# A two-layer hybrid encoder in fp32r: latent projections first and freed from the norm of x, first squares summed by TensorE, a searched order of instructions

## The chip, the cores and the metric

One core of one Trainium2 chip runs the whole program. The metric is the device time of one execution in microseconds (us). The kernel before was timed three times; its median is 1267.3 us. One execution was also profiled, and all rows below come from that one.

## The reference

Sequence 512, width 1024, two layers, all in float32. Each layer does, on x (512 x 1024):

```python
proj = rms_norm(x, attn_norm[l]) @ w_in[l]
h_mla, h_diff, h_ch = jnp.split(proj, [IN_MLA, IN_MLA + IN_DIFF], axis=-1)
o_mla = rms_norm(mla_attention(h_mla, ...), mla_out_norm[l])    # 6 heads, latents of 256 (q) and 128 (k, v)
o_diff = diff_attention(h_diff, ...)                            # 6 heads, two softmaxes each
o_ch = rms_norm(chunk_attention(h_ch, ...), chunk_out_norm[l])  # 4 heads
x = x + jnp.concatenate([o_mla, o_diff, o_ch], axis=-1) @ w_out[l]
x = x + conv_ffn(rms_norm(x, ffn_norm[l]), ...)                 # 2 x 2816 wide, causal conv of 3, silu gate
```

and a last `rms_norm`. In `mla_attention` the latents `c_q` and `c_kv` are normed a second time, `rms_norm(c_q, q_norm) @ w_uq`. That second norm takes the first one out again: with r the row factor of the first norm and a the raw product, `rms_norm(r a)` is `a / sqrt(mean(a²) + eps / r²)`, and `eps / r²` is `eps (mean(x²) + eps)`.

## The kernel before

x lies transposed: eight tiles `xs[k]` of 128 channels x 512 positions. Every float32 factor is split in two fp32r halves (high, and the rest), and every product is three fp32r matmuls: high x high, high x low, low x high. A weight unit of 128 output channels therefore takes 24 matmuls of 512 columns (`proj`, L748), which add into one of three PSUM banks named psproj.

The norm factor r of x is not in the operands. `Gain.split` (L712) makes the halves of gain times x, the matmuls run on them, and `unit` (L868) multiplies the finished bank by r when it empties it; until r is there the bank stays taken (`Gain.finish`, L732). r itself comes from `Gain.square` (L720): ScalarE (ACT) squares a tile, VectorE (DVE) adds it to a sum, and `rstd` (L671) splits the sum (`split_sums`), sums it over the partitions with two matmuls against ones into a bank named pspt, and `rsqrt` (L691) makes r from it: Ln, Exp and Square on ACT, two instructions on DVE.

Weights come as jobs in a fixed order (`ORDER`, L81): q0 and q1 are the query latents, kv the key/value latent, kr the rotary key; e, v, u, d, c, g are the other projections; a and b the two parts of the output projection. `weights` (L536) loads a raw tile over the sync queue (SP), ACT casts the high half, and the low half is made either by DVE (a subtraction) or by ACT and an adding DMA of GpSimd (POOL), `pool.dma_start(..., accum_op=ALU.add)`. Job v (unit "uv") and the jobs u need the normed latents; the first 384-wide matmuls of the program are those of uv, in `latent_values` (L988). `latent` (L967) empties a latent's bank with r and norms it again.

The order of the instructions is planned in the kernel itself. Every instruction is first recorded (`Engine.__getattr__`, L361, so nearly all rows carry L361 as their line), with a cost and with lags between engines (`Clock.issue`, `lag`). `Clock.emit` (L332) then schedules the record backwards and forwards four times and keeps the order whose last instruction starts earliest. Each engine executes its own queue in that order.

Of the kernel before, what the change touches and what calls it, by code (L numbers as in the profile page):

```python
# [40 lines left out]
for t, n in (("wh", 2), ("wl", 3), ("xg", 8), ("lat", 3), ("kmla", 4), ("x", 6), ("v", 5), ("pt", 2), ("nhl", 1)):  # L41
    RINGS_R[t] = list(range(NR, NR + n))
    NR += n
# [16 lines left out]
for t, w, n in (("wraw", 1024, 2), ("P", GCOLS, 2), ("P1", GCOLS, 1), ("ev", S, 2), ("rb", S, 1), ("acc", S, 1),  # L60
# [10 lines left out]
RINGS_F["set"] = (S, [ol0[0], o0[4], o0[5]])  # L71
# [4 lines left out]
ROUNDS = 4  # L76
# [4 lines left out]
ORDER = "q0 kv kr q1 e0 v e1 u0 u1 u2 d0 d1 d2 e2 c0 c1 g0 g1 a0 a1 a2 a3 a4 a5 a6 a7 b0 b1"  # L81
# [39 lines left out]
class Clock:  # L121
# [6 lines left out]
    TO_PE = dict(act=0.265, dve=0.252, pool=0.203, pe=0.0)  # L128

# [70 lines left out]
    def settle(self):  # L200
# [15 lines left out]
        while ready:  # L216
# [13 lines left out]
    def issue(self, eng, op, outs, ins, func, emit):  # L230
# [62 lines left out]
    def lag(self, a, eng):  # L293

        return 0.0 if a.eng == eng else self.TO_PE[a.eng] if eng == "pe" else 0.197 if a.eng == "pe" else 0.157 if eng == "pool" else 0.13

    def list_schedule(self, rank, needs, users, forth):
# [8 lines left out]
        for _ in self.ops:  # L306
# [11 lines left out]
            if o.size and forth:  # L318
                line = max(line, end + 0.65) + o.size / 360e3
            for d in users(o):  # L320
                a, b = (o, d) if forth else (d, o)
                if a.size:
                    r = line + 0.9 + o.late if forth else end + 1.55 + a.late + a.size / 360e3
# [8 lines left out]
    def emit(self):  # L332


        start = self.list_schedule(list(range(len(self.ops))), lambda o: o.needs, lambda o: o.users, True)
        best = start
        for _ in range(ROUNDS):
            back = self.list_schedule([-(start[o.n] + o.cost) for o in self.ops], lambda o: o.users, lambda o: o.needs, False)
            start = self.list_schedule([-(back[o.n] + o.cost) for o in self.ops], lambda o: o.needs, lambda o: o.users, True)
            best = min(best, start, key=max)  # L340
# [136 lines left out]
def encoder(ctx, tc, xT, pos_row, pos_col, wflat, small, lam, relx, cst, out):  # L477
# [58 lines left out]
    def weights(l, name, run, finish, gate=lambda: True):  # L536
        o, c = offs[l, name]
        runs = [(0, c // 2), (c // 2, c)] if l == 0 and not work.jobs else [(0, c)]
# [4 lines left out]
        def fetch():  # L543
            raw = T("wraw")
            part(raw, *runs[0])
            if len(runs) > 1:
                rest_of_first.append(lambda: part(raw, *runs[1]))
            return raw

        def halves(raw):  # L550
# [8 lines left out]
            for a, b in runs:  # L559
                act.copy(wh[:, a:b], raw[:, a:b])  # L560
# [941 lines left out]
```

## Time and profile before

| | |
|---|---|
| runs | 1266.69, 1267.3, 1270.7 us; median 1267.3 |
| the profiled execution | 1264.97 us, span of its instructions 1263.2 us |
| busy share of the span | PE 97%, weight loads 78%, DVE 70%, ACT 56%, POOL 10% |
| granted TensorE clock, mean | 0.99 of 2.4 GHz |
| the two attention parts | about 0 to 285 us and 625 to 901 us |
| the two gated MLPs | about 285 to 625 us and 901 to 1250 us |

The profiled execution is 2.3 us below the median. PE's busy share counts a matmul from its start to its modelled end, so matmuls overlap in it, and a stretch at 100% need not be at TensorE's peak; the number of matmuls in a stretch tells more.

### The profile page before, as it was taken

How to read it: one execution, taken by the hardware profiler on the slowest of the kernel's cores; microseconds unless marked ns; L12 is line 12 of the kernel's file. 1: busy time of each engine (PE TensorE's matmuls, PEld its weight loads, DVE VectorE, ACT ScalarE, POOL GpSimd, SP SyncE). 2: the span in 40 equal slices, each digit the busy share in tenths (PEclk: the TensorE clock that was granted, in tenths of full speed). 3: DMA queues.
4: the chain of work that ended last, by engine and by line, in shares of the span. 5: the costliest groups of instructions: out<-in, count | busy, mean ns of one | idle time of the engine just before them, and what ended most of it. 6: DMA issues, size and time to landing. Idle time of an engine off the chain costs nothing.

```text
span 1263.2 us, 15644 instructions
## 1 busy us (share of the span) xinstructions
PE 1219.3 (97%) x5591; PEld 990.1 (78%) x5591; DVE 882.3 (70%) x1608; ACT 710.9 (56%) x1224; POOL 127.7 (10%) x186
## 2 busy tenths in 40 slices
PE   6899999989999999999999999999999999999996
PEld 4788776768888888888877878777788888888885
DVE  7798899668776347775457979975877643677644
ACT  6798887755443134444367878976644422444443
POOL 1113320140000000000011143101300000000001
PEclk9899999999999999999999999999999999999998
DMA  6657961543232332323366597526232233323232
GB/s 183 145 143 150 232 139 42 130 117 102 98 101 81 99 107 96 101 90 92 103 144 140 134 219 172 123 68 162 89 101 94 86 95 118 95 92 100 78 100 90
DMA packets 51470, 146.86 MB, mean 116 GB/s; under 512 B 6464, under 2 KB 9536, under 8 KB 51392
## 3 DMA queue, kind: packets, MB, share of 16 engines
q1 hardware_dynamic: 36992, 106.27, 26.4%
q0 software_dynamic: 14400, 39.59, 16.9%
q8 instruction: 44, 0.72, 0.2%
q14 instruction: 34, 0.28, 0.1%
HBM read 104.16 MB, written 2.10 MB: 84 GB/s over the span
## 4 chain that ended last, share of the span: by engine, by line
PE 80%; DVE 9%; ACT 5%; DMA 3%; issue 1%; SPq 0%; DVEq 0%; ACTq 0%
PE psproj L361 70%; DVE af L361 5%; PE pss L361 4%; PE pspt L361 3%; DVE ar L361 3%; PE psav L361 3%; ACT ar L361 3%; ACT af L361 3%; DMA af<-in_wflat 2%; DVE xa L361 1%; DMA xa<-in_xT 0%; DMA ar<-af 0%; DVE rl L361 0%; SPq L361 0%; ACT L860 0%
## 5 line engine op out<-in xcount | busy, mean ns | idle before, releaser
L361 PE MATMUL psproj<-ar 128*128 128x512 f32 (+1 forms) x4595 | 1107.9, 393 | 25.4 <-ACT ar L361 9.0
L361 PEld LDWEIGHTS psproj<-ar 128*128 128x128 f32 x4595 | 852.6, 189 | 204.8 <-ACT ar L361 22.3
L361 ACT CAST ar<-af 128x1024 fp32r<-128x1024 f32 (+3 forms) x338 | 272.9, 822 | 222.6 <-PE psproj L361 194.7
L361 DVE TENSOR_TENSOR ar<-af,ar 128x512 fp32r<-128x512 f32 (+3 forms) x257 | 240.7, 939 | 174.1 <-ACT ar L361 173.4
L361 DVE SCALAR_TENSOR_TENSOR af<-af,sma 128x511 f32<-128x511 f32 (+1 forms) x192 | 143.0, 750 | 47.6 <-ACT af L361 44.3
L361 ACT ACTIVATE af<-af,sma 128x512 f32<-128x512 f32 x88 | 71.9, 818 | 141.5 <-DVE af L361 141.5
L361 POOL DMA_DIRECT2D ar<-af x62 | 54.7, 883 | 664.1 <-ACT ar L361 586.2
L361 ACT ACTIVATE af<-af,mn 128x128 f32<-128x128 f32 (+3 forms) x176 | 98.3, 559 | 16.8 <-DVE mn L361 16.1
L361 ACT ACTIVATE af<-af 128x512 f32<-128x512 f32 (+1 forms) x106 | 66.1, 624 | 66.5 <-DVE af L361 65.4
L361 PE MATMUL pss<-ar 128*128 128x128 f32 (+9 forms) x336 | 88.5, 338 | 2.2 <-DVE mn L361 2.1
L361 DVE TENSOR_TENSOR af<-psproj,af 128x512 f32<-128x512 f32 x114 | 77.9, 685 | 14.7 <-PE psproj L361 14.1
L361 DVE TENSOR_TENSOR af<-af 128x512 f32<-128x512 f32 (+1 forms) x78 | 52.9, 678 | 36.4 <-ACT af L361 35.6
L361 PEld LDWEIGHTS pss<-ar 128*128 128x128 f32 (+2 forms) x336 | 55.9, 188 | 22.0 <-DVE mn L361 7.7
L361 ACT ACTIVATE ar<-af 128x1024 fp32r<-128x1024 f32 (+3 forms) x62 | 59.1, 953 | 20.9 <-DMA af<-in_wflat 15.6
L361 PE MATMUL psav<-ar 128*128 128x512 f32 (+3 forms) x256 | 66.7, 334 | 2.7 <-DVE ar L361 1.9
L361 DVE TENSOR_TENSOR ar<-pspt,ar 128x512 fp32r<-128x512 f32 (+1 forms) x106 | 63.0, 606 | 4.3 <-ACT ar L361 2.7
L361 PE MATMUL pspt<-ident,af 128*128 128x128 f32 x360 | 63.6, 278 | 1.4 <-DVE af L361 1.1
L361 PEld LDWEIGHTS pspt<-ident,af 128*128 128x128 f32 x360 | 45.6, 141 | 18.3 <-DVE af L361 5.1
L361 DVE TENSOR_TENSOR xa<-xa,psproj 128x512 f32<-128x512 f32 (+1 forms) x65 | 43.1, 672 | 19.7 <-PE psproj L361 19.6
L361 PEld LDWEIGHTS psav<-ar 128*128 128x128 f32 x256 | 45.0, 189 | 12.0 <-DVE ar L361 4.3
L361 DVE CUSTOM_DVE_ANT_0 af<-pss,dist 128x384 f32<-128x384 f32 (+2 forms) x96 | 45.5, 484 | 5.1 <-PE pss L361 4.9
L361 POOL DMA_DIRECT2D ar<-ar x78 | 43.0, 588 | 35.3 <-PE pss L361 26.0
(65 smaller groups left out, 537.2 us busy)
## 6 DMA issues: line engine op xcount, KB each, us to landing
af<-in_wflat SPq DMA_DIRECT2D x127, 512.0 KB, 3.4
ar<-af POOLq DMA_DIRECT2D x38, 512.0 KB, 5.1
af<-in_wflat SPq DMA_DIRECT2D x48, 384.0 KB, 3.0
af<-in_wflat SPq DMA_DIRECT2D x38, 320.0 KB, 2.9
ar<-ar POOLq DMA_DIRECT2D x72, 128.0 KB, 4.8
ar<-af POOLq DMA_DIRECT2D x16, 384.0 KB, 4.2
xa<-in_xT SPq DMA_DIRECT2D x8, 256.0 KB, 5.7
af<-in_relx SPq DMA_DIRECT2D x8, 256.0 KB, 2.8
```

The lines of the kernel that those rows point to most:

```text
L361: self.clock.issue(self.name, op, outs, ins + aps, func, lambda: fn(*args, **kw))
```

## The change

- The latents go first: kv, q0, q1, then kr. Their banks are emptied by a plain ACT copy as soon as the matmuls are done, without r. In place of r, the second norm gets `eps / r²`: `rstd` and the new `squares` keep `me = EPS / d * sum(x²)` (an ACT copy of the PSUM sum), and DVE adds `d / P * me` to the sum of the latent's squares.
- In layer 0, DVE no longer adds the squares of x: each squared tile goes as a float32 matmul against ones into one PSUM bank, with one more for eps.
- The first three jobs of the program are loaded and split in halves, their high halves cast by DVE and their low halves subtracted by DVE; the first x tile is loaded ahead of the first weights. The ring of high halves grows from two tiles to three. The descriptor scratch of POOL's DMAs is halved.
- The last scaling of x is three DVE instructions for each half, in place of eight on DVE and POOL.
- The planner gets a lag between instructions of one engine (`SELF`), other prices for DMAs, and sixty rounds disturbed by random numbers in place of four; it keeps the order whose last instruction ends earliest.

```diff
-for t, n in (("wh", 2), ("wl", 3), ("xg", 8), ...
+for t, n in (("wh", 3), ("wl", 3), ("xg", 8), ...
...
-ROUNDS = 4
+ROUNDS = 60
...
-ORDER = "q0 kv kr q1 e0 v e1 u0 u1 u2 d0 d1 d2 e2 c0 c1 g0 g1 a0 a1 a2 a3 a4 a5 a6 a7 b0 b1"
+ORDER = "kv q0 q1 kr e0 v e1 u0 u1 u2 d0 d1 d2 e2 c0 c1 g0 g1 a0 a1 a2 a3 a4 a5 a6 a7 b0 b1"
...
+    SELF = dict(pe=0.0, act=0.14, dve=0.125, pool=0.3, sp=0.0)
...
-                o.line = free["line"] = max(free["line"], o.end + 0.65) + o.size / 360e3
-                o.end = o.line + 0.9 + o.late
+                o.line = free["line"] = max(free["line"], o.end + 0.65) + o.size / 300e3
+                o.end = o.line + 0.6 + o.late
...
-            late = (2.3 if size < 1 << 18 else 4.5) * (eng == "pool")
+            late = (2.6 if size < 1 << 18 else 1.8) * (eng == "pool")
...
+        rnd = random.Random(0)
+        best = start = forth([o.n for o in self.ops])
         for _ in range(ROUNDS):
...
+            late = back([rnd.gauss(0, 0.5) - start[o.n] - o.cost for o in self.ops])
+            start = forth([-(late[o.n] + o.cost) for o in self.ops])
+            best = min(best, start, key=span)
+            if span(start) > span(best) + 0.3:
+                start = best
...
-        runs = [(0, c // 2), (c // 2, c)] if l == 0 and not work.jobs else [(0, c)]
+        runs = [(0, c // 2), (c // 2, c)] if l == 0 and len(work.jobs) < 3 else [(0, c)]
...
-                act.copy(wh[:, a:b], raw[:, a:b])
-            if name[0] == "f" or clock.now() == 0:
+                (act.copy if len(runs) == 1 else dve.tensor_copy)(wh[:, a:b], raw[:, a:b])
+            if name[0] == "f" or len(runs) > 1:
...
+            if keep is not None:
+                act.activation(keep, pb, AF.Copy, scale=EPS / d)
...
+        def squares(self):
+
+            pb = PT("pt")
+            pe.matmul(pb, lhsT=ones.bitcast(F32), rhs=eps_t.to_broadcast([P, S]), start=True, stop=False)
+            for k in range(KD):
+                q = tmp("sq")
+                act.activation(q, self.xs[k], AF.Square)
+                pe.matmul(pb, lhsT=ones.bitcast(F32), rhs=q, start=False, stop=k == KD - 1)
+            self.me = tmp("me")
+            act.activation(self.me, pb, AF.Copy, scale=EPS / self.d)
+            self.then(rsqrt(pb, self.d, tmp("y"), tmp("s"), lambda: tmp("rb")))
...
-                rstd(self.acc, self.d, P, ones, self.then, "rb")
+                self.me = tmp("me")
+                rstd(self.acc, self.d, P, ones, self.then, "rb", keep=self.me)
...
-            def finish(job, acc, rb):
+            def finish(job, acc):
                 f = tmp("ol")
-                dve.tensor_tensor(f, acc, rb, op=ALU.mult)
+                act.copy(f, acc)
+                close_bank()
...
-                rstd(sumsq(fs), d, P, ones, then)
-            return unit(name, gain_a, finish)
+                acc = sumsq(fs)
+                dve.scalar_tensor_tensor(acc, gain_a.me, d / P, acc, op0=ALU.mult, op1=ALU.add)
+                rstd(acc, d, P, ones, then, eps=0.0)
+            return weights(l, name, lambda w: proj(gain_a.tiles, w, []), finish)
...
-        for k, eng in enumerate((dve, dve, pool, dve, dve, dve, pool, dve)):
-            x = xs[k][:, hs]
-            eng.tensor_tensor(x, x, r, op=ALU.mult)
-            if k in OUT:
-                x = xa.rearrange("p (k s) -> p k s", k=KD)[:, done : k + 1, hs]
-                sp.dma_start(out[:, done : k + 1, hs], x)
-                done = k + 1
+        for k in OUT:
+            x = tiles[:, done : k + 1, hs]
+            dve.tensor_tensor(x, x, r[:, None, :].to_broadcast([P, k + 1 - done, HALF]), op=ALU.mult)
+            sp.dma_start(out[:, done : k + 1, hs], x)
+            done = k + 1
...
-    nc = _bacc.Bacc("TRN2", target_bir_lowering=False, num_devices=1, dynamic_dma_scratch_size=8192)
+    nc = _bacc.Bacc("TRN2", target_bir_lowering=False, num_devices=1, dynamic_dma_scratch_size=4096)
```

What this does to the queues is shown at three places. In each row stand the instruction, what it writes and reads, and the shape it writes (`x12` is twelve of them in a row); ar are the fp32r tiles, af the float32 ones, xa is x, psproj, pspt and pss are PSUM banks.

PE at the start of layer 0, before: from the end of the second unit to the first 384-wide matmuls, which are uv's. Of the units, the three psproj banks hold q0, kv and kr first, then q1 (the first psproj_63 rows here) and e0 (psproj_64, 24).

```order
L361 MATMUL psproj_64<-ar 128x512 x13
L361 MATMUL pspt_68<-ar,ones 128x512
L361 MATMUL psproj_65<-ar 128x512 x12
L361 MATMUL pspt_68<-ar,ones 128x512
L361 MATMUL psproj_65<-ar 128x512 x4
L361 MATMUL psproj_63<-ar 128x512 x12
L361 MATMUL pspt_69<-ar,ones 128x512 x2
L361 MATMUL psproj_63<-ar 128x512 x12
L361 MATMUL psproj_64<-ar 128x512 x24
L361 MATMUL psproj_65<-ar 128x384 x3
```

The same in the change: kv in psproj_63, q0 in psproj_64, q1 in psproj_65, then kr (psproj_63) and e0 (psproj_64); `pspt_68<-af,ones` are the float32 squares.

```order
L371 MATMUL psproj_63<-ar 128x512 x7
L371 MATMUL pspt_68<-af,ones 128x512 x2
L371 MATMUL psproj_64<-ar 128x512 x5
...
L371 MATMUL psproj_65<-ar 128x512 x13
L371 MATMUL psproj_63<-ar 128x512 x2
L371 MATMUL pspt_69<-ar,ones 128x512 x2
L371 MATMUL psproj_65<-ar 128x512
L371 MATMUL psproj_63<-ar 128x512 x11
L371 MATMUL psproj_65<-ar 128x512 x3
L371 MATMUL psproj_63<-ar 128x512 x3
L371 MATMUL psproj_64<-ar 128x512 x11
L371 MATMUL psproj_65<-ar 128x384 x2
```

Counted over the whole start, uv's first matmul had 112 matmuls of units and 4 of norms before it; now it has 99 and 2, and nine float32 ones.

DVE where layer 0 goes from the output projection to the MLP, before: `xa<-xa,psproj` empties a bank of the output projection into x, `ar<-xa,sma,ar` makes the low half of a new x tile (`Gain.split`), `ar<-af,ar 128x1024` the low half of an MLP weight.

```order
L361 TENSOR_TENSOR xa<-xa,psproj_64 128x512
L361 SCALAR_TENSOR_TENSOR ar<-xa,sma,ar 128x512 x3
L361 TENSOR_TENSOR ar<-af,ar 128x1024
L361 TENSOR_TENSOR xa<-xa,psproj_65 128x512
L361 TENSOR_TENSOR xa<-xa,psproj_63 128x512
L361 TENSOR_TENSOR xa<-xa,psproj_64 128x512
L361 SCALAR_TENSOR_TENSOR ar<-xa,sma,ar 128x512
L361 TENSOR_TENSOR xa<-xa,psproj_65 128x512
```

The same in the change.

```order
L371 SCALAR_TENSOR_TENSOR ar<-xa,sma,ar 128x512 x2
L371 TENSOR_TENSOR ar<-af,ar 128x1024
L371 TENSOR_TENSOR xa<-xa,psproj_63 128x512
L371 TENSOR_TENSOR xa<-xa,psproj_64 128x512
L371 SCALAR_TENSOR_TENSOR ar<-xa,sma,ar 128x512
L371 TENSOR_TENSOR xa<-xa,psproj_65 128x512
L371 SCALAR_TENSOR_TENSOR ar<-xa,sma,ar 128x512
L371 TENSOR_TENSOR xa<-xa,psproj_63 128x512
L371 SCALAR_TENSOR_TENSOR ar<-xa,sma,ar 128x512
L371 TENSOR_TENSOR xa<-xa,psproj_64 128x512
```

The last four bank emptyings now alternate with the splits.

DVE at the end of the program, before: `xa<-xa,psproj_65` and `psproj_63` add the two halves of the last output tile, 256 positions each.

```order
L361 SCALAR_TENSOR_TENSOR af<-pspt_68,af 128x256
L361 SCALAR_TENSOR_TENSOR af<-af 128x256
L361 TENSOR_TENSOR xa<-xa,af 128x256 x2
L361 TENSOR_TENSOR xa<-xa,psproj_63 128x256
L361 TENSOR_TENSOR xa<-xa,af 128x256 x4
L361 SCALAR_TENSOR_TENSOR af<-pspt_69,af 128x256
L361 SCALAR_TENSOR_TENSOR af<-af 128x256
L361 TENSOR_TENSOR xa<-xa,af 128x256 x6
```

The same in the change.

```order
L371 TENSOR_TENSOR xa<-xa,psproj_65 128x256
L371 TENSOR_TENSOR xa<-xa,psproj_63 128x256
L371 SCALAR_TENSOR_TENSOR af<-pspt_68,af 128x256
L371 SCALAR_TENSOR_TENSOR af<-pspt_69,af 128x256
L371 SCALAR_TENSOR_TENSOR af<-af 128x256 x2
L371 TENSOR_TENSOR xa<-xa,af 128x2x256 x2
L371 TENSOR_TENSOR xa<-xa,af 128x3x256 x4
```

The first half's norm and scaling stood between the two additions; now both halves go through every step side by side, and on PE the last matmuls of psproj_65 stand among those of psproj_63.

## Rows read from the trace of the kernel before

**Rows 1.** The page's busy times: share of the span, number of instructions.
```profile
PE 1219.3 (97%) x5591; PEld 990.1 (78%) x5591; DVE 882.3 (70%) x1608; ACT 710.9 (56%) x1224; POOL 127.7 (10%) x186
```
**Rows 2.** Busy us by stretch (count): PE, PEld, DVE, ACT, POOL; granted clock, DMA share, GB/s.
```profile
300.00:400.00 100.00, 100.00 (x443) 82.81 (x442) 73.71 (x95) 44.90 (x58) 0.00 (x0) 1.00 0.29 93
20.00:40.00 20.00, 11.89 (x44) 9.22 (x43) 15.82 (x33) 12.64 (x17) 3.71 (x8) 0.74 0.55 126
60.00:260.00 200.00, 194.25 (x979) 155.04 (x978) 167.83 (x445) 162.54 (x352) 41.44 (x65) 1.00 0.61 140
660.00:680.00 20.00, 16.04 (x76) 12.32 (x75) 14.90 (x28) 13.83 (x26) 5.18 (x8) 1.00 0.82 191
680.00:880.00 200.00, 196.24 (x972) 154.94 (x971) 163.91 (x431) 160.59 (x348) 39.79 (x63) 0.99 0.62 141
```
**Rows 3.** Timeline of the start: start, length, engine, instruction, [idle before <- releaser].
```profile
4.74 0.63 ACT L361 ACTIVATE af<-xa 128x512 f32<-128x512 f32 x1
...
19.57 0.69 DVE L361 TENSOR_TENSOR af<-af 128x512 f32<-128x512 f32 x1 [0.79 <-ACT af L361]
...
25.14 0.68 DVE L361 SCALAR_TENSOR_TENSOR ar<-af,ar 128x512 fp32r<-128x512 f32 x1
...
31.09 0.60 ACT L361 ACTIVATE af<-pspt 128x512 f32<-128x512 f32 x1
...
33.77 0.69 DVE L361 SCALAR_TENSOR_TENSOR af<-af 128x512 f32<-128x512 f32 x1
...
35.41 4.88 PE L361 MATMUL psproj<-ar 128*128 128x512 f32 x12 [8.11 <-DVE af L361]
```
**Rows 4.** Tile psproj by stretch: ns min/median/max, first and last start (12:15, 15:18, 36:39, 44:60).
```profile
L361 PE MATMUL psproj<-ar x8: 628/628/792, 11.5 to 14.8; 128*128 128x512 f32 x8
L361 PE MATMUL psproj<-ar x14: 387/391/628, 14.4 to 18.0; 128*128 128x512 f32 x14
L361 PE MATMUL psproj<-ar x9: 628/628/763, 35.4 to 39.0; 128*128 128x512 f32 x9
L361 ACT CAST ar<-psproj x5: 460/481/582, 49.5 to 59.3; 128x384 fp32r<-128x384 f32 x4, 64x512 fp32r<-64x512 f32 x1
```
**Rows 5.** Timeline of layer 0's step from output projection to MLP, and 272 to 274 us.
```profile
268.57 2.29 DVE L361 TENSOR_TENSOR ar<-af,ar 128x1024 fp32r<-128x1024 f32 x1
...
271.51 6.87 PE L361 MATMUL psproj<-ar 128*128 128x512 f32 x22 [2.54 <-DVE xa L361]
...
272.00:274.00 2.00, 2.00 (x6) 1.59 (x5) 1.31 (x3) 2.00 (x5) 0.00 (x0) 0.50 0.66 242
```
**Rows 6.** Timeline of layer 1's start.
```profile
654.12 0.69 DVE L361 SCALAR_TENSOR_TENSOR af<-pspt,af 128x512 f32<-128x512 f32 x1 [5.19 <-ACT af L361]
...
662.63 1.89 PE L361 MATMUL psproj<-ar 128*128 128x384 f32 x8 [1.59 <-DMA ar<-af]
```
**Rows 7.** Timeline of the end, and 1254 to 1255 us.
```profile
1247.34 0.40 PE L361 MATMUL pspt<-ar,ones 128*128 128x256 f32 x2
...
1247.58 0.60 PE L361 MATMUL pspt<-af,ones 128*128 128x256 f32 x2
...
1247.83 2.86 PE L361 MATMUL psproj<-ar 128*128 128x256 f32 x21
...
1255.54 3.15 DVE L361 TENSOR_TENSOR xa<-xa,af 128x256 f32<-128x256 f32 x6
...
1254.00:1255.00 1.00, 0.00 (x0) 0.00 (x0) 0.38 (x1) 0.56 (x2) 0.00 (x0) 0.82 1.01 341
```
**Rows 8.** Instructions by shape: busy us, mean ns of one | idle before.
```profile
L361 DVE TENSOR_TENSOR af<-psproj,af 128x512 f32<-128x512 f32 x114 | 77.9, 685 | 14.7 <-PE psproj L361 14.1
L361 DVE TENSOR_TENSOR ar<-af,ar 128x768 fp32r<-128x768 f32 x32 | 30.6, 958 | 39.0 <-ACT ar L361 38.6
```
**Rows 9.** DMA issues from 100 to 180 us: number, KB each, median us to landing.
```profile
ar<-af POOLq DMA_DIRECT2D x9, 512.0 KB, 5.2
af<-in_wflat SPq DMA_DIRECT2D x8, 512.0 KB, 5.0
```

More of the change, by code (lines that the diff above doesn't have):

```diff
@@ L2 @@
 import math
+import random
 from contextlib import ExitStack
@@ L40 @@
 RINGS_R, NR = {}, 0
-for t, n in (("wh", 2), ("wl", 3), ("xg", 8), ("lat", 3), ("kmla", 4), ("x", 6), ("v", 5), ("pt", 2), ("nhl", 1)):
+for t, n in (("wh", 3), ("wl", 3), ("xg", 8), ("lat", 3), ("kmla", 4), ("x", 6), ("v", 5), ("pt", 2), ("nhl", 1)):
     RINGS_R[t] = list(range(NR, NR + n))
@@ L59 @@
 RINGS_F, NF = {}, 0
-for t, w, n in (("wraw", 1024, 2), ("P", GCOLS, 2), ("P1", GCOLS, 1), ("ev", S, 2), ("rb", S, 1), ("acc", S, 1),
+for t, w, n in (("wraw", 1024, 2), ("P", GCOLS, 2), ("P1", GCOLS, 1), ("ev", S, 2), ("rb", S, 1), ("me", S, 1), ("acc", S, 1),
                 ("y", S, 1), ("s", S, 1), ("o", S, 6), ("ol", S, 1)):
@@ L318, in list_schedule @@
             if o.size and forth:
-                line = max(line, end + 0.65) + o.size / 360e3
+                line = max(line, end + 0.65) + o.size / 300e3
             for d in users(o):
@@ L322, in list_schedule @@
                 if a.size:
-                    r = line + 0.9 + o.late if forth else end + 1.55 + a.late + a.size / 360e3
+                    r = line + 0.6 + o.late if forth else end + 1.25 + a.late + a.size / 300e3
                 else:
@@ L332, in emit @@
     def emit(self):
-        start = self.list_schedule(list(range(len(self.ops))), lambda o: o.needs, lambda o: o.users, True)
-        best = start
-        for _ in range(ROUNDS):
-            back = self.list_schedule([-(start[o.n] + o.cost) for o in self.ops], lambda o: o.users, lambda o: o.needs, False)
-            start = self.list_schedule([-(back[o.n] + o.cost) for o in self.ops], lambda o: o.needs, lambda o: o.users, True)
-            best = min(best, start, key=max)
+        forth = lambda rank: self.list_schedule(rank, lambda o: o.needs, lambda o: o.users, True)
+        back = lambda rank: self.list_schedule(rank, lambda o: o.users, lambda o: o.needs, False)
+        span = lambda start: max(t + o.cost for t, o in zip(start, self.ops))
+        rnd = random.Random(0)
+        best = start = forth([o.n for o in self.ops])
+        for _ in range(ROUNDS):
+            late = back([rnd.gauss(0, 0.5) - start[o.n] - o.cost for o in self.ops])
[3 more added lines that the diff above has]
+                start = best
         for o in sorted(self.ops, key=lambda o: (best[o.n], o.n)):
@@ L545, in fetch @@
             part(raw, *runs[0])
-            if len(runs) > 1:
+            if work.jobs[0].raw is None:
                 rest_of_first.append(lambda: part(raw, *runs[1]))
+            elif len(runs) > 1:
+                part(raw, *runs[1])
             return raw
@@ L669, in add_square, with rstd @@
             eng.tensor_tensor(acc, acc, q, op=ALU.add)
-    def rstd(acc, d, group, lhs, then, ring="acc"):
+    def rstd(acc, d, group, lhs, then, ring="acc", eps=EPS, keep=None):
         hl = pair("nhl")
-        split_sums(acc, hl, d, group)
+        split_sums(acc, hl, eps * d / group)
         def rest():
@@ L974, in finish, with norm @@
                     job.set(None)
-                    return
+                else:
+                    gain_a.finish(lambda: norm(job))
+            def norm(job):
                 def then(r):
@@ L1229, in layer @@
                 gain_a.split(k)
-                if k == 4:
-                    work.jobs[1].load()
-            for k in range(KD):
-                gain_a.square(k)
+                if k in (1, 4):
+                    work.jobs[1 + k // 4].load()
+            gain_a.squares()
             setup_rope()
```

19 lines of the change are left out of this document (11 added, 8 removed).

## The prediction

> **What bounds the kernel now.** I read the page's busy times first, then the busy time by stretch, then the timeline wherever a stretch has fewer matmuls than PE can run. PE is busy for 97% of the span [rows 1], so the first question is where that is a real limit. From 300 to 400 us it runs 443 matmuls in 100 us, one each 0.2257 us, without a gap [rows 2]. That is the pace of both MLPs, together some 690 us, and the change removes no matmul there; nothing can be won in them. What remains are the starts of the two layers, their attention parts, the step from the output projection to the MLP, and the end. I take them in order of time.
>
> The start has the largest hole. From 20 to 40 us PE runs 44 matmuls where 88 would fit [rows 2]. The timeline says why: the sum of squares takes its last addition at 19.57, but the low half of that sum is made only at 25.14, Ln starts only at 31.09, and the factor r is written at 33.77; PE, whose three banks all wait for r, stands from 27.3 to 35.41 [rows 3]. After that idle time the granted clock is 0.74 over the stretch [rows 2], and matmuls take 628 ns in place of 387 [rows 4]; these are the two levels, 1.2 and 2.4 GHz. The matmuls before about 15 us take 628 ns too [rows 4].
>
> In the attention parts there is less to see: from 60 to 260 us PE idles 5.8 us in all, from 680 to 880 us 3.8 us, with DVE at 84 and 82% and ACT at 81 and 80% [rows 2]. Two holes have a name. PE waits 2.54 us at 271.51 because DVE, in the middle of emptying the output projection's banks, makes a weight half that takes 2.29 us; the clock falls behind it, and the next 2 us hold 6 matmuls in place of 9 [rows 5]. And from 660 to 680 us PE idles 4.0 us [rows 2] around the first matmuls of uv, which wait for an adding DMA [rows 6]. From the last psproj matmul, which ends at 1247.83 + 2.86 = 1250.69, to the end of the span at 1263.2 there are 12.5 us [rows 7].
>
> **The change, part by part.** *Start of layer 0.* I compare one event, ACT taking the first 384-wide block of uv, now at 49.5 [rows 4]. Until then PE must run 112 + 4 matmuls, 116 x 0.2257 = 26.2 us; 23.3 us are lost. Afterwards 99 + 2 stand in front of it, 22.8 us, and nine float32 ones. A float32 matmul of 256 columns shows as a pair with 0.60 us, two fp32r ones as 0.40 [rows 7]; of the latter 0.11 is each one's pace and some 0.19 the way through, so the float32 one costs 0.41, and 0.82 at 512 columns. The one for eps needs no data and lies before the first x tile; eight are 6.6 us. PE can begin once the first tile is squared: that square now takes 0.63 from 4.74 behind a weight cast [rows 3], later it is ACT's first work; I take 5.0. At full pace 29.4 us end at 34.4. If PE stays at the low level until about 15, as it does now, half of those ten microseconds is lost, 5.2: 39.6.
>
> Two other queues must keep up. DVE has 40 instructions from the last x tile at about 16 us to the low half of the kv latent, 19.7 us at 0.69 for two full operands [rows 8] and less for narrow ones; with its waits for two Ln chains I arrive at 38.7. ACT ends its part at about 38. So nobody waits for r, the block is taken at about 40.5, 9.0 earlier; 13 matmuls are now behind it in place of ahead, 2.9 us. **The gain is 6.1 us.** It is 3 if DVE's chain is 3 us later than counted, and 8 if the clock rises at 10 us, as PE is given work earlier.
>
> *Output projection to MLP, layer 0.* The bank emptyings alternate with the splits; the 2.29 us instruction still stands once in front of two of them, but later ones no longer pile up. The wait of 2.54 and three matmuls' worth of low clock, 0.7, go, and I leave 0.2 for a short wait: 3.0. Ends: 0 and 3.2.
>
> *Start of layer 1.* kv is first, its bank is emptied without r, and its norm needs only the sum. The chain that waited 5.19 us for ACT [rows 6] begins one unit of 24 matmuls earlier. What is late next is uv's weight half, an adding DMA, whose issue behind ACT also moves up. I take 3.0 of the 4.0 us; ends: 0 and 4.
>
> *The end.* Before, the first half's norm and two scalings run beside the second half's matmuls. Now both halves arrive together. I walk from the last psproj matmul: additions end at +0.7, squares at 1.1, two scalings on ACT come ahead of Ln and end at 2.2, two Ln at 3.0, four Exp and Square at 4.7, DVE's four norm instructions at 6.2, then two scalings of 512 elements (0.69 each) and four of 768 (0.96 each, [rows 8]): 11.4. Behind DVE's last instruction, which now ends at 1255.54 + 3.15 = 1258.69, the span lasts 4.5 us [rows 7]; I keep that. It makes 15.9 in place of 12.5, less 0.4 because the first half's norm matmuls no longer stand among the psproj ones: **3.0 us lost.** Ends 1.5 and 6; all output transfers now fall together, but 2.1 MB at the 341 GB/s of [rows 7] are 6.1 us and fit beside the scalings.
>
> *The rest of the order.* Sixty rounds and new lags reorder the attention parts. Reading the queues does not give me a time. It can win at most the 5.8 + 3.8 us of idle time, and I bound a loss at 12 from the rival below; I take 2 won, near the lower end, since the pieces there are short and DVE and ACT are full.
>
> *At nothing:* four copies of `me` (two of them never read) and six bank emptyings moved from DVE (685 ns, [rows 8]) to ACT, hidden by the matmuls of the other units in flight; without that cover 0.6 each. The third high-half buffer and the halved DMA scratch cost nothing unless POOL's queue fills, which no row shows.
>
> Sum: -6.1 - 3.0 - 3.0 + 3.0 - 2.0 = -11.1. Against the profiled execution's 1264.97 that is 1253.9; that execution lies 2.3 under the median, so I forecast **1256.2 us** for the median. About 0.3%, 3.8 us, is what a measurement of this kernel can tell from no change.
>
> **The rivals.** *First: the order wins far more.* All idle time of the two attention parts goes, and the clock rises early: another 10 us, **1246**. For it: the new planner prices transfers as the trace has them. Against: DVE at 84%.
>
> *Second: the early start is used up before the MLP.* Heads are paced by DVE and ACT, which are loaded evenly; if a later bound (the adding DMAs between 100 and 180 us) sets the pace, 6.1 is lost again: **1262.3**.
>
> *Third: the search does nothing elsewhere.* Only start and end change: -6.1 + 3.0, **1264.2**. Against it: the queues of all engines differ in hundreds of places.
>
> *Fourth, slower: transfers planned too tightly.* From issue to landing the old planner charges 8.1 us for an adding DMA of 512 KB, the new one 5.4 (0.55, 0.65, 524 KB at 300 GB/s, 0.6, 1.8), and the trace shows 5.2 to landing in the busy stretch; but a plain load, charged 3.4, lands there after 5.0 [rows 9]. PE executes in order, so a weight that lands late stops everything behind it. In each layer 17 such transfers are issued in a stretch like this one; if half of the 34 stop PE for 0.9 us, 15.3 are lost: **1271.5**. It decides the sign from 0.88 us a stop. Against it: the plan puts all transfers on one line, so part of 5.0 is in it.
>
> The adding DMAs land after 5.2 us [rows 9]. The Trainium skill, page "DMA: Bandwidth & Descriptors", section on the anatomy of one DMA on the SWDGE path, fits such a DMA by 2.0 us plus bytes at 436 GB/s, which makes 3.2 us an estimate for 512 KB. By that rule every adding DMA would be there 2 us ahead of the plan, the fourth rival would rest on the plain loads alone and its chance would halve, to 0.08, with the sum as it is; the trace contradicts it, so I go by 5.2.
>
> **How the numbers follow.** Forecast 0.40 (all of it faster), first rival 0.15 (faster), second 0.15 (0.09 faster, 0.06 same), third 0.13 (0.03 and 0.10), fourth 0.17 (0.03 same, 0.14 slower): faster 0.67, same 0.19, slower 0.14. The forecast's own range, from its ends at start and finish, is 1251 to 1261. The range that leaves out 2 in 10 runs from the first rival, 1246, to just short of the fourth, 1270.
>
> **What would show it.** Right: uv's first block is taken at 39 to 42, PE has no idle piece of 8 us in the start and no clock at 0.50 from 30 to 38; no 2.5 us wait on xa at the first MLP; some 16 us from the last psproj matmul to the end of the span. Wrong: PE stands in front of uv for DVE; new waits of PE on `af<-in_wflat` or `ar<-af`; fewer than 443 matmuls per 100 us in an MLP.

## The result: 0.8% slower, with the start won as forecast

The change takes 1275.9 us (median of five runs) against 1266.7 for the kernel before: ratio 1.0076, 95% interval 1.0051 to 1.0101. The forecast was 1256.2 with a range of 1246 to 1270. The profiled execution has the median's own time, with a span of 1274.1 us, 10.9 more than before. Executions more than 1.5% above the fastest of their kernel, some of e1, e10 and e12, are left out of the ratios, and e10's profile is such a one.

The page after: busy shares as in [rows 1], DVE slightly less, and the chain of work that ended last (shares of the span by engine, then by line).

```profile
PE 1230.7 (97%) x5607; PEld 996.6 (78%) x5607; DVE 860.9 (68%) x1601; ACT 707.7 (56%) x1228; POOL 122.5 (10%) x181
...
PE 77%; DMA 10%; DVE 4%; ACT 4%; issue 3%; POOL 0%; SPq 0%; DVEq 0%; ACTq 0%; POOLq 0%
PE psproj L371 68%; DMA af<-in_wflat 6%; DMA ar<-af 4%; PE pspt L371 3%; PE pss L371 3%; PE psav L371 3%; ACT ar L371 2%; DVE af L371 2%; DVE ar L371 2%; ACT af L371 2%; DVE xa L371 1%; DMA xa<-in_xT 0%; POOL ar L371 0%; SPq L371 0%; ACT xa L371 0%
```

DMAs are now 10% of that chain: weight loads (`af<-in_wflat`) and adding DMAs (`ar<-af`). The same line of the kernel before, and of two experiments further down: e5 puts the old price of the adding DMAs back in the plan, e13 keeps the change's order and makes these DMAs small.

```profile
PE 80%; DVE 9%; ACT 5%; DMA 3%; issue 1%; SPq 0%; DVEq 0%; ACTq 0%
...
PE 85%; DVE 6%; ACT 4%; DMA 4%; issue 2%; DVEq 0%; ACTq 0%; POOLq 0%; SPq 0%
...
PE 92%; DVE 3%; ACT 2%; DMA 1%; issue 0%; POOL 0%; DVEq 0%; SPq 0%; ACTq 0%
```

Next the busy time by stretch, to lay beside [rows 2] (columns: stretch, length, PE, PEld, DVE, ACT, POOL busy with their instructions, clock, DMA share, GB/s).

```profile
20.00:40.00 20.00, 20.00 (x86) 15.73 (x85) 15.52 (x35) 16.54 (x26) 3.19 (x7) 1.00 0.45 116
60.00:260.00 200.00, 191.56 (x940) 150.84 (x940) 158.34 (x430) 156.16 (x344) 39.39 (x63) 0.97 0.59 132
300.00:400.00 100.00, 100.00 (x442) 82.78 (x442) 73.34 (x97) 47.34 (x60) 0.00 (x0) 1.00 0.30 95
660.00:680.00 20.00, 17.01 (x72) 13.10 (x72) 14.08 (x23) 11.10 (x20) 3.93 (x6) 0.95 0.83 187
680.00:880.00 200.00, 190.59 (x953) 153.00 (x952) 161.13 (x435) 156.78 (x346) 39.72 (x63) 0.98 0.61 133
...
132.00:136.00 4.00, 0.96 (x6) 0.46 (x4) 1.44 (x4) 3.90 (x11) 0.00 (x0) 0.89 0.70 153
136.00:140.00 4.00, 4.00 (x13) 3.42 (x14) 3.14 (x8) 2.23 (x5) 0.00 (x0) 0.50 0.39 129
140.00:144.00 4.00, 4.00 (x17) 3.28 (x17) 2.25 (x7) 2.55 (x7) 2.99 (x6) 0.76 0.41 81
```

The hole of the start is full: 86 matmuls from 20 to 40 us where 44 were. The MLP keeps its pace. The loss lies in the attention parts: 39 matmuls fewer from 60 to 260 us, and 19 fewer from 680 to 880. At 132 us PE stands for 3 of 4 us, and the next 4 us run at a clock of 0.50, which is 1.2 GHz, with 13 matmuls.

A stretch of the same clock times does not hold the same work in two kernels. So I cut each trace at the start of its k-th psproj matmul (4595 in every kernel) and took the time between cuts, in us:

| psproj matmuls | before | after | e5 | e13 |
|---|---|---|---|---|
| start to 150 | 57.7 | 52.0 | 50.2 | 50.6 |
| 150 to 300 | 64.6 | 65.0 | 64.2 | 62.7 |
| 300 to 400 (MLA to difference heads, layer 0) | 32.5 | 36.4 | 33.2 | 30.4 |
| 400 to 800 (other heads, output projection) | 143.6 | 148.2 | 138.8 | 139.8 |
| 800 to 2250 (MLP) | 328.7 | 328.7 | 328.7 | 328.7 |
| 2250 to 2450 (start of layer 1) | 55.5 | 53.9 | 58.1 | 50.0 |
| 2450 to 2550 | 49.1 | 49.9 | 48.6 | 49.0 |
| 2550 to 2700 (MLA to difference heads, layer 1) | 50.1 | 55.4 | 50.1 | 46.1 |
| 2700 to 3000 | 112.0 | 113.7 | 110.2 | 110.4 |
| 3000 to 4550 (MLP) | 350.8 | 350.8 | 350.8 | 350.8 |
| 4550 to the end | 18.7 | 20.0 | 19.6 | 20.1 |

So 5.7 us are won at the start and lost again in the third and fourth row (3.9 + 4.6). In layer 1, 5.3 go where the difference heads begin. (The 10.6 + 13.6 us that e1's expectation names for the two passages are larger; the table, taken at the same matmuls in both kernels, is what I go by.)

Part of the loss goes with TensorE's clock. Busy time and granted clock from 60 to 290 and 680 to 905 us, before, in the change and in e5:

```profile
60.00:290.00 230.00, 221.71 (x1090) 176.84 (x1089) 190.62 (x471) 179.63 (x377) 53.34 (x72) 0.99 0.58 137
680.00:905.00 225.00, 220.45 (x1073) 173.50 (x1072) 185.78 (x454) 176.40 (x372) 51.18 (x70) 0.99 0.59 137
...
60.00:290.00 230.00, 218.15 (x1047) 171.81 (x1047) 178.38 (x451) 172.55 (x367) 51.61 (x71) 0.96 0.57 130
680.00:905.00 225.00, 213.80 (x1050) 170.73 (x1049) 181.55 (x459) 173.52 (x370) 51.06 (x72) 0.98 0.61 134
...
60.00:290.00 230.00, 226.82 (x1106) 179.51 (x1105) 191.34 (x467) 180.74 (x378) 52.63 (x71) 1.00 0.57 136
680.00:905.00 225.00, 220.03 (x1075) 174.94 (x1076) 185.88 (x448) 174.56 (x363) 51.85 (x69) 1.00 0.58 137
```

The clock that is missing, times the length, is 9.2 + 4.5 = 13.7 us in the change, 4.6 before and nothing in e5, each good to some 2 us, as the column has two digits. As an estimate, then, up to 9 of the 15 us that the change loses behind its start go because TensorE runs at the low level behind its stops, and the rest are the stops. It is no more than that, since a slow clock costs nothing where PE waits for other engines anyway.

What PE waits for in the attention parts is mostly the output of ACT or DVE; ACT in turn waits for weight loads. From the list of what ACT waited for, in the same two stretches (us in total, times, longest):

```profile
ACT ar L371 <- DMA af<-in_wflat: 13.4, 8, 4.0
...
ACT ar L371 <- DMA af<-in_wflat: 15.8, 5, 5.4
```

That is 29.2 us; before, the same two rows give 4.0 and 7.7. The chain of work from 733 to 767 us shows how a load comes late (start, us, what):

```profile
727.17 6.33 DMA ar<-af
...
733.57 8.07 DMA af<-in_wflat
...
741.71 7.57 issue
...
749.29 4.87 DMA ar<-af
...
754.21 10.68 DMA af<-in_wflat
...
765.00 1.54 ACT ar L371 x2
...
766.58 0.80 PE psav L371
```

The 7.57 us are put down to no wait that the view knows. ACT's timeline shows other work in them; it comes to the half that the adding DMA needs only at 747.68:

```profile
747.68 1.04 ACT L371 ACTIVATE ar<-af 128x1024 fp32r<-128x1024 f32 x1
```

The rest is a loop. There are two raw tiles; an adding DMA reads its raw tile, so the next load of that tile waits on SP until the addition has landed; the load then has to land before ACT can cast, and PE waits for ACT's output (4.42 us, until 766.58). One turn of addition and load takes 6.33 + 8.07 = 14.4 us here, the next 4.87 + 10.68 = 15.6. The new planner prices it at 5.4 + 3.4 = 8.8, the old one at 8.1 + 3.4 = 11.5. The adding DMAs and loads, and the `ar<-ar` DMAs of POOL that stack parts of heads into one tile, from 728 to 768 us and from 96 to 150 us (count, KB, median us to landing):

```profile
ar<-ar POOLq DMA_DIRECT2D x21, 128.0 KB, 6.9
ar<-af POOLq DMA_DIRECT2D x5, 512.0 KB, 6.3
af<-in_wflat SPq DMA_DIRECT2D x4, 512.0 KB, 7.2
...
ar<-ar POOLq DMA_DIRECT2D x27, 128.0 KB, 5.7
ar<-af POOLq DMA_DIRECT2D x6, 512.0 KB, 6.4
af<-in_wflat SPq DMA_DIRECT2D x5, 512.0 KB, 5.1
```

6.3 + 7.2 is 13.5 and 6.4 + 5.1 is 11.5, against the 8.8 that the plan allows. In the kernel before, the same matmuls run from 726 to 759 and from 104 to 150 us, and there the landings give 5.6 + 5.2 = 10.8 and 6.0 + 5.3 = 11.3, against 11.5 planned.

### The profile page after: what moved, and what is told of

The parts are those of the page before. It is cut to its first block, busy times and chain, and to the rows that moved or that the text cites. A ratio compares the mean times of both kernels' runs of the same rounds, so it can differ in the third digit from the quotient of the medians.

```text
span 1274.1 us, 15618 instructions
## 1 busy us (share of the span) xinstructions
PE 1230.7 (97%) x5607; PEld 996.6 (78%) x5607; DVE 860.9 (68%) x1601; ACT 707.7 (56%) x1228; POOL 122.5 (10%) x181
## 4 chain that ended last, share of the span: by engine, by line
PE 77%; DMA 10%; DVE 4%; ACT 4%; issue 3%; POOL 0%; SPq 0%; DVEq 0%; ACTq 0%; POOLq 0%
PE psproj L371 68%; DMA af<-in_wflat 6%; DMA ar<-af 4%; PE pspt L371 3%; PE pss L371 3%; PE psav L371 3%; ACT ar L371 2%; DVE af L371 2%; DVE ar L371 2%; ACT af L371 2%; DVE xa L371 1%; DMA xa<-in_xT 0%; POOL ar L371 0%; SPq L371 0%; ACT xa L371 0%
## 5 line engine op out<-in xcount | busy, mean ns | idle before, releaser
L371 ACT CAST ar<-af 128x512 fp32r<-128x512 f32 (+4 forms) x333 | 271.2, 821 | 295.9 <-PE psproj L371 161.0
L371 DVE TENSOR_TENSOR ar<-af,ar 128x512 fp32r<-128x512 f32 (+4 forms) x260 | 240.9, 930 | 140.7 <-PE psproj L371 95.6
L371 DVE TENSOR_TENSOR af<-psproj,af 128x512 f32<-128x512 f32 x108 | 73.9, 687 | 79.6 <-PE psproj L371 79.2
L371 PE MATMUL pss<-ar 128*128 128x128 f32 (+7 forms) x336 | 89.3, 339 | 2.9 <-DVE mn L371 2.9
L371 ACT ACTIVATE af<-af 128x512 f32<-128x512 f32 (+1 forms) x106 | 65.4, 621 | 30.4 <-DVE af L371 29.5
L371 PE MATMUL pspt<-ident,af 128*128 128x128 f32 x360 | 69.2, 282 | 6.0 <-DVE ar L371 5.4
L371 DVE TENSOR_TENSOR af<-af 128x512 f32<-128x512 f32 (+2 forms) x71 | 48.0, 676 | 31.6 <-ACT af L371 30.9
```

The costliest lines, as they stand in the source:

```text
L371: self.clock.issue(self.name, op, outs, ins + aps, func, lambda: fn(*args, **kw))
```

## The experiments

Each time is a median, with the ratio to the kernel before (run on the same chip, 1264.9 to 1267.3 us).

### Which part of the change: prices, search or the program

Put back in the change: the DMA prices (e1), the search (e2), the whole planner (e3). e4 is the kernel before with the whole new planner, e3's edits the other way round.

```diff
# e1 and e3 (o.line likewise in list_schedule)
-                o.line = free["line"] = max(free["line"], o.end + 0.65) + o.size / 300e3
-                o.end = o.line + 0.6 + o.late
+                o.line = free["line"] = max(free["line"], o.end + 0.65) + o.size / 360e3
+                o.end = o.line + 0.9 + o.late
-            late = (2.6 if size < 1 << 18 else 1.8) * (eng == "pool")
+            late = (2.3 if size < 1 << 18 else 4.5) * (eng == "pool")
# e2 and e3 (and no gauss, no return to best)
-ROUNDS = 60
+ROUNDS = 4
-            best = min(best, start, key=span)
+            best = min(best, start, key=max)
# e3 besides
-    SELF = dict(pe=0.0, act=0.14, dve=0.125, pool=0.3, sp=0.0)
+    SELF = dict(pe=0.0, act=0.0, dve=0.0, pool=0.0, sp=0.0)
```

> The changed kernel (1275.9 us against 1266.7 for the kernel before, ratio 1.0076) with the planner's old DMA prices put back (line rate 360, 0.9 after the line, late 2.3 and 4.5 us); search, lags and all edits of the program stay. Theory P (the cheaper DMA prices let loads and adding DMAs be planned too late where the MLA heads pass to the difference heads, in both layers): most of the loss of 10.6 + 13.6 us at the head before the first difference head goes, and the time comes to about 1256 to 1263 us, ratio .990 to .997. Theory S (the disturbed search settles on an order that the chip does not run as planned, whatever the prices): within 0.3% of the change, 1272 to 1280. Theory E (the early start and the new weight order themselves bring the loads together there): also 1272 to 1280.

> The changed kernel with the old search put back (four undisturbed rounds, the order whose last instruction starts earliest); new prices, lags and all edits stay. Theory P (prices): stays slow, 1270 to 1282 us, ratio over 1.003. Theory S (search): back to 1256 to 1264. Theory E (early start): stays slow, 1270 to 1280.

> The edits of the program alone: the changed kernel with the old planner (old DMA prices, no lag between instructions of one engine, four undisturbed rounds). Theories P and S: the start's win stands and the middle runs as before, so 1257 to 1264 us, ratio .992 to .998. Theory E (the early start or the new weight order makes the loss at the passage from MLA to difference heads, or the smaller descriptor scratch slows the DMAs of GpSimd): over 1270.

> The kernel before with the new planner alone (new DMA prices, lags, sixty disturbed rounds), program unchanged. Theories P and S: slower than before by what the change lost in its middle and more, 1272 to 1285 us. Theory E: about as before, 1262 to 1268, since the program's start and order of weights are the old ones.

Measured: e1 1266.0 (1.0006, 0.9992 to 1.0021), e2 1268.9 (1.0029, 1.0013 to 1.0045), e3 1263.5 (0.9985, 0.9971 to 0.9999), e4 1271.4 (1.0049, 1.0031 to 1.0068). The program's edits do not make the loss (e3): the new planner alone slows the old program too (e4). The halved descriptor scratch is in e3 too, so it makes no loss either. Old prices bring back 9.9 us and the old search 7, so neither theory P nor S stands alone: e1 stayed above what P expected, and e2 fell below P's range without reaching S's. e4 lies just under the 1272 that both had as their lower end.

### Which price, and how much is a draw

```diff
# e5 (and e9, e10)
-            late = (2.6 if size < 1 << 18 else 1.8) * (eng == "pool")
+            late = (2.3 if size < 1 << 18 else 4.5) * (eng == "pool")
# e6 (likewise in list_schedule)
-                o.end = o.line + 0.6 + o.late
+                o.end = o.line + 0.9 + o.late
# e7 and e9; 2 in e8 and e10
-        rnd = random.Random(0)
+        rnd = random.Random(1)
```

> The changed kernel with one price put back: the adding DMAs land late by 4.5 us in the plan in place of 1.8 (2.3 in place of 2.6 for the small ones); line rate 300 and the 0.6 us stay as changed. Theory P1 (it is the adding DMA's price that lets the plan run too tight): as the run with all old prices, 1262 to 1269 us, ratio .998 to 1.003. Theory P2 (it is the plain load's price): stays at 1271 to 1280. Theory S2 (every order that the disturbed search makes is a draw between about 1262 and 1277, whatever the prices): anywhere in that.

> The changed kernel with the plain price put back: line rate 360 and 0.9 us after it; the adding DMAs keep 1.8 us. Theory P1: stays slow or gets slower, since the plan is tighter still, 1271 to 1282 us. Theory P2: 1262 to 1269. Theory S2: anywhere between 1262 and 1277.

> The changed kernel with another seed for the disturbed search (1 in place of 0), nothing else. Theory P (new prices): as slow as the change, 1270 to 1280 us, because every search under these prices fills the same slack. Theory S2 (a draw): could as well be 1262 to 1268. The planner's own span is 1.3 us shorter than with seed 0; the chip is not expected to follow it.

> The changed kernel with seed 2. As for seed 1: theory P 1270 to 1280 us, theory S2 anywhere between 1262 and 1277; the planner's own span is 0.5 us longer than with seed 0.

> The run of 1255.0 us (the changed kernel with the adding DMAs late by 4.5 us in the plan), with seed 1. Theory P1 (the price of the adding DMAs decides, a seed scatters by some 4 us around it): 1251 to 1264 us, below the same seed under the changed price (1263.6). Theory S2 (a draw whatever the price; 1255.0 was luck): around the mean of all draws so far, 1264 to 1272.

> The same with seed 2. Theory P1: 1251 to 1264 us, below the same seed under the changed price (1268.1). Theory S2: 1264 to 1272.

| seed | addition late by 1.8 | late by 4.5 |
|---|---|---|
| 0 | 1275.9 (1.0076, 1.0051 to 1.0101) | e5 1255.0 (0.9925, 0.9902 to 0.9949) |
| 1 | e7 1263.6 (0.9983, 0.9965 to 1.0001) | e9 1259.7 (0.9951, 0.9934 to 0.9968) |
| 2 | e8 1268.1 (1.0021, 1.0006 to 1.0036) | e10 1260.6 (0.9956, 0.9940 to 0.9972) |
| mean | 1269.2 | 1258.4 |

e6 stays at 1271.7 (1.0039, 1.0023 to 1.0056). So it is the addition's price, not the load's: with it put back, each seed gets faster, by 20.9, 3.9 and 7.5 us, 10.8 in the mean. (The edit also sets the small POOL DMAs, under 256 KB, from 2.6 to 2.3; no run does that alone.) All three runs with the old price lie below all three with the new one, which would come about once in twenty times if the price did nothing. But a seed moves the cheap-priced kernel by 12 us, which theory P had not expected (e7 and e8 both fell below its 1270): seed 0 of the change, 6.7 above the mean of its row, was a bad draw on top. e5 is below what any theory had expected, 1262 at the least, and 1255 is a good draw of its row, 3.4 below the mean. In e5 ACT's two waits for loads are

```profile
ACT ar L371 <- DMA af<-in_wflat: 9.7, 3, 5.6
...
ACT ar L371 <- DMA af<-in_wflat: 9.1, 2, 5.5
```

18.8 us, of which the longest single wait is no shorter than in the change. The additions themselves land no sooner than in the change (6.7 us from 96 to 150); what differs is the order around them. PE's own waits in the two stretches are 3.0 and 5.2 us in e5, against 11.7 and 11.1 in the change and 7.9 and 4.2 before.

### A longer price, and the old program searched

e11 sets 6.0 us for the addition in the change; e12 is the kernel before with new line rate, lags and search, but its own 4.5 us.

> The changed kernel, seed 0, with the adding DMAs late by 6.0 us in the plan, more than either kernel has. Theory P1, in its strong form (any slack that the plan leaves ahead of an adding DMA is paid back on the chip): no slower than with 4.5, 1250 to 1258 us, though the planner's own span grows by 15 us. In its weak form (the price has to fit): 1258 to 1266, as loads that are pulled forward push others back. Theory S2: anywhere between 1255 and 1276.

> The program of the kernel before with the changed planner in all but the price of the adding DMAs (new line rate, lags, sixty disturbed rounds; late 4.5 us). Against the run of 1255.0 us it lacks only the edits of the program. If the search is worth what that run gained and the edits are worth the 1.9 us that they gave under the old planner: 1256 to 1262 us. If the edits are worth the 6 to 8 us that the start gains: 1261 to 1267, no faster than the kernel before.

Measured: e11 1267.2 (1.0013, 0.9997 to 1.0029), e12 1270.0 (1.0021, 0.9998 to 1.0043). e11 lies above both forms of theory P1 (inside S2's wide range), e12 above both of its ranges. Too long a price loses again, with one seed: e11 needs 60.3 us for the row "start of layer 1", the most of all profiles used. PE waits there mostly for DVE and ACT (1.0 of 6.8 us for additions); why was not followed up. e12's interval is wide, and it shows only that the search alone does not make e5.

### The additions themselves, with every order held

The plan is left as it is; only what an addition of 512 columns or more transfers is cut to an eighth of its columns, so that the low halves made in this way lack most of their correction. The edit stands where an instruction is recorded.

```diff
-            self.clock.issue(self.name, op, outs, ins + aps, func, lambda: fn(*args, **kw))
+            def emit():
+                if "accum_op" in kw and args[0].ap[-1][1] >= 512 and len(args[0].ap) == 2:
+                    n = args[0].ap[-1][1] // 8
+                    return fn(args[0][:, :n], args[1][:, :n], **kw)
+                return fn(*args, **kw)
+            self.clock.issue(self.name, op, outs, ins + aps, func, emit)
```

> The changed kernel with its order on every engine as it is, but the adding DMAs of weights of 512 columns and more move only the first eighth of the columns (the low halves of the other weights stay minus the high half, so the products lack their correction). The plan still counts them in full. Theory L (in the change these DMAs land later on the chip than planned, and what waits for them, directly or through the raw tile that they hold, makes the loss): the time falls by 12 to 20 us, to 1256 to 1264. Theory O (the order of the computing engines is bad by itself, the DMAs only happen to be near): it falls by under 5 us, 1271 to 1276.

> The same edit in the kernel before, whose plan leaves each adding DMA 2.7 us more. Theory L: little is lost to them there, so it falls by 0 to 7 us, 1259 to 1267, and the change with the same edit is no slower than this. Theory O: it falls by as much as the change does, and the change stays about 9 us slower than this.

> The same edit in the run of 1255.0 us (the changed kernel with the adding DMAs late by 4.5 us in the plan). Theory L: 0 to 5 us less, 1250 to 1255, and the difference to the change with the same edit is under 8 us where it was 21. Theory O: the difference between the two stays about 15 to 21 us.

Measured: the change 1241.3 (e13: 0.9803, 0.9780 to 0.9825), before 1258.3 (e14: 0.9937, 0.9919 to 0.9954), e5 1248.5 (e15: 0.9863, 0.9838 to 0.9888). The change gets shorter by 34.6 us, the kernel before by 8.9, e5 by 6.5. This settles it for theory L against O: with additions that land early, the order that was slowest is the fastest. But L had expected 12 to 20 us; all three runs came out below its ranges, most of all e13. The edit takes away two things at once, the additions' late landing and their traffic, and these runs do not divide the loss between the two. In e13 ACT's wait for loads in layer 0 is

```profile
ACT ar L375 <- DMA af<-in_wflat: 2.7, 2, 2.4
```

and in layer 1 it is 0.3. The matmuls that the change runs from 728 to 768 us stand from 706 to 737 in e13, and the landings there are

```profile
ar<-ar POOLq DMA_DIRECT2D x21, 128.0 KB, 5.3
af<-in_wflat SPq DMA_DIRECT2D x4, 512.0 KB, 4.6
ar<-af POOLq DMA_DIRECT2D x4, 64.0 KB, 3.8
```

so in this passage the loads (7.2 in the change) and the stack DMAs (6.9) land sooner as well, though they are unchanged. In layer 0 (94 to 140 us, the change's 96 to 150) only the stack DMAs do, 4.8 against 5.7; the loads take 5.3 against 5.1. That the additions' traffic had slowed the loads thus fits layer 1 and not layer 0. The Trainium skill, page "DMA: Bandwidth & Descriptors", section "Issuing engines are not separate DMA queues", says that DMAs started by SP or GpSimd run on the same 16 engines and interleave; the trace agrees in layer 1 (7.2 to 4.6 us) and shows nothing of it in layer 0. PE from 60 to 260 and 660 to 860 us in e13 (the change has 940 matmuls in the first of these stretches):

```profile
60.00:260.00 200.00, 196.47 (x989) 158.01 (x989) 167.57 (x442) 164.63 (x355) 45.57 (x68) 0.99 0.37 93
...
660.00:860.00 200.00, 196.67 (x998) 158.77 (x997) 170.31 (x448) 164.08 (x356) 42.76 (x65) 1.00 0.40 95
```

### Prices fitted to the busy stretch

```diff
# likewise in list_schedule
-                o.end = o.line + 0.6 + o.late
+                o.end = o.line + 1.5 + o.late
-            late = (2.6 if size < 1 << 18 else 1.8) * (eng == "pool")
+            late = (4.0 if size < 1 << 18 else 3.5) * (eng == "pool")
```

e16 is the change with these, e18 the same with seed 1, e17 the old program under this planner.

> The changed kernel with all three prices fitted to what its own profile shows at the passage from the MLA heads to the difference heads (96 to 150 us), in place of the whole program's medians: 1.5 us after the line (in place of 0.6), adding DMAs late by 3.5 us more (1.8), the small ones by 4.0 (2.6). Theory P1: as with the price of 4.5, 1253 to 1262 us. If a longer price only pulls loads forward into each other (as 6.0 us did): 1262 to 1268.

> The program of the kernel before with the changed planner and the fitted prices of the run of 1255.3 us. If the edits of the program (latents first and without r, squares on PE, the halved first loads) are worth the 6 to 11 us that the start and the runs with small adding DMAs suggest: 1261 to 1267. If they are worth 1.9 us, as under the old planner: 1255 to 1259.

> The run of 1255.3 us (the changed kernel with fitted prices) with seed 1. If the price decides and a seed scatters by 3 us: 1252 to 1261, below the kernel before. If 1255.3 was luck: 1262 to 1270.

Measured: e16 1255.3 (0.9916, 0.9896 to 0.9937), e18 1257.9 (0.9940, 0.9926 to 0.9953), e17 1261.9 (0.9968, 0.9958 to 0.9978). e16 and e18 came out in the ranges of the theory that the price decides, e17 in the range forecast for edits worth 6 to 11 us. The turn is priced at 12.3 us here. e5 and e16 beat the kernel before by some 11 us and the change by 20; they cannot be told apart. Under this planner the edits of the program are worth 4.0 to 6.6 us (e17, one seed, against e18 and e16), the planner with fitted prices some 4 (e17 against before).

All runs by what the planner asks for one turn of addition (512 KB) and load, with the sum of ACT's waits for loads (60 to 290 and 680 to 905 us) and the end of the planner's own schedule, which it works out as the program is built and which is no chip time:

| turn, us | runs | ACT's waits | plan's end | measured less plan's end |
|---|---|---|---|---|
| 8.8 | after, e2, e4, e6, e7, e8 | 22.8 to 33.3 | 1201.8 to 1215.4 | 53 to 70 |
| 11.5 | before, e1, e3, e5, e9, e10, e12 | 9.8 to 21.4 (without e10) | 1216.4 to 1221.7 | 38 to 48 |
| 12.3 | e16, e17, e18 | 4.6 to 15.6 | 1227.7 to 1236.2 | 26 to 30 |
| 13.0 | e11 | 8.2 | 1232.2 | 35 |

ACT's waits follow the price of the turn, but they do not rank the times: e12 has 9.8 us of them and takes 1270.0, e5 18.8 and 1255.0. Nor does the price alone: with 11.5 us for the turn, times run from 1255.0 to 1270.0, and e1 differs from e5 only in the plain price of every transfer (360 and 0.9 in place of 300 and 0.6, the same sum for a turn) and takes 11.0 more.

The change's plan ends 10.8 us earlier than that of the kernel before (1207.7, 1218.6), and the chip runs it 9.2 us longer. The search's share is seen beside e2: sixty disturbed rounds in place of four bring the plan's end from 1215.4 to 1207.7, 7.7 us earlier, and the chip's time up by 7.0. What they found was time that the new price had promised and the chip did not have.

## Why the prediction was wrong, point by point

**Start, -6.1: right.** uv's first block is taken at 41.62 us (49.5 in [rows 4], 40.5 forecast), PE has no hole from 20 us on to it, and the clock stays at 1.00 from 20 to 40; the first cut gives -5.7. From the timelines of ACT and PE:

```profile
41.62 0.85 ACT L371 CAST ar<-psproj 128x384 fp32r<-128x384 f32 x2
...
32.11 10.64 PE L371 MATMUL psproj<-ar 128*128 128x512 f32 x46
```

**Output projection to MLP, -3.0: wrong.** The wait of 2.54 us [rows 5] is still there, now 2.69. Reading DVE's order, I took the weight half's new place to be enough. But its cause is another one now: the half itself takes 1.23 us in place of 2.29, and comes late because its load does. The chain of work in front of this wait is the loop of addition and load again (first fence). With small additions (e13) the wait on xa is 0.5 us, in e5 1.0.

```profile
256.76 5.37 DMA ar<-af
...
262.18 5.63 DMA af<-in_wflat
...
267.89 1.05 ACT ar L371
...
268.97 1.23 DVE ar L371
```

PE there, and at the start of layer 1:

```profile
270.84 11.52 PE L371 MATMUL psproj<-ar 128*128 128x512 f32 x42 [2.69 <-DVE xa L371]
...
662.32 3.46 PE L371 MATMUL psproj<-ar 128*128 128x384 f32 x15 [0.56 <-DMA ar<-af]
...
677.56 2.31 PE L371 MATMUL psproj<-ar 128*128 128x512 f32 x5 [1.86 <-DMA ar<-af]
```

**Start of layer 1, -3.0: too much.** The 5.19 us [rows 6] were DVE's wait for ACT and had not stopped PE. What stopped it at uv was an adding DMA, and still does, as "late next" had it: 0.56 us in place of 1.59 at 662 us, then 1.86 at 677 (the last two rows above), with 72 matmuls from 660 to 680 us where 76 were [rows 2]. The row "start of layer 1" of the cuts won 1.6.

**The end, +3.0: right in kind, +1.9 in size,** within its ends. The last psproj matmul ends at 1254.83 + 4.84 = 1259.67, 14.4 us before the end of the span (12.5 in [rows 7]); DVE's scalings begin 4.5 us behind it, where I had 6.2, and take 4.76 for the six of them, where I had 5.2; from their end at 1268.97 to the end of the span it is 5.1 us, where I had kept 4.5:

```profile
1254.83 4.84 PE L371 MATMUL psproj<-ar 128*128 128x256 f32 x39
...
1264.21 4.76 DVE L371 TENSOR_TENSOR xa<-xa,af 128x512 f32<-128x512 f32 x6
```

**The rest of the order, -2.0: here the prediction failed.** Between the first cut and the last, the table sums to +15.1 (3.9 + 4.6 + 5.3 + 1.7 and the other rows add to -0.4), with the two terms above in it, beyond even the bound of 12. It is the fourth rival's mechanism (15.3 us in its own sum, with a chance of 0.17), which the prediction talked down. It held the addition's 5.2 us against the new 5.4 as a price that fits, and met the load, 5.0 against 3.4, with "the plan puts all transfers on one line, so part of 5.0 is in it". But an addition and a load follow each other through one raw tile, so the two prices had to be added. [Rows 9] gave 5.2 + 5.0 = 10.2 against 8.8, short by 1.4 on each turn, and the old price's surplus of 2.9 on the addition had been paying for the load. e13 shows that the additions are the cause (34.6 us less), e5, e9 and e10 that their price in the plan decides (10.8 us less in the mean of three seeds); the other half of the 20.9 us between the change and e5 is the draw. Where I went wrong in form: I had the rival as 17 stops of PE of 0.9 us each. The loss is a few chains, with ACT's longest stop 4.0 us in layer 0 and 5.4 in layer 1, and the clock behind them: 0.50 after the stop at 132 us, and up to 9 us of loss in all by the estimate above, for which the rival had no term. That its sum comes near the measured loss is therefore luck. The second rival's picture, a start that is used up before the MLP, is also what happened, but through these chains: the 600th psproj matmul starts 2.6 us later than before (248.6, 246.0).

The page's rule that I weighed (the Trainium skill, "DMA: Bandwidth & Descriptors", anatomy of one DMA on the SWDGE path) would give an estimate of 3.2 us for 512 KB. The additions took 6.3 and 6.4 in the two passages. For the 64 KB additions of e13 the rule's estimate is 2.2; they landed after 2.4 us from 94 to 140 us and after 3.8 us from 706 to 737. So it comes near in one of these four places and is short in the others.

Open: why one seed costs 12 us more than another at the same price, why e1 is 11.0 us slower than e5, and why e11 and e12 are as slow as they are.

## What to carry to other kernels

When a planner's costs are changed, add the costs along each resource that goes round (tile, addition, load, tile) and hold that sum against the busiest stretch, not each cost against its own median over the program: an overcharge in one may be the only cover for an undercharge in the other. A search that is judged by its own model can gain by that model's errors, as the sixty rounds did here, so compare the plan's gain with the chip's, and run more than one seed before a single order is believed. An edit is worth what it gives under the planner that it will be used with: the same edits gave some 2 us under the old planner (e3, ratio 0.9985), then 4.0 to 6.6.

## What was not expected of the hardware

Unchanged DMAs shared the additions' delay in one passage of layer 1: with additions of 64 in place of 512 KB, a 512 KB load of the same work landed after 4.6 instead of 7.2 us, and a 128 KB stack DMA after 5.3 instead of 6.9. In layer 0 the loads gained nothing (5.3 against 5.1). A single load took 10.68 us in that passage of the change, against a median of 3.4 over the whole program.

Short stops cost more than their own length. Behind PE's stops of some 3 us in the attention parts (at 132, 2.8 until 225.44, 2.69 until 270.84) the granted clock falls to 0.50. From 60 to 290 and 680 to 905 us PE's waits sum to 22.8 us in the change and the missing clock to 13.7; before it was 12.1 and 4.6.
